# Moving attention steps later behind a head's results, and a fourth early pair with low parts on GpSimd

## The chip, the cores and the metric

The kernel runs on one core of a Trainium2 chip. The metric is the time of one execution on the device in microseconds (us). A core has TensorE (PE), which multiplies; VectorE (DVE) and ScalarE (ACT), which do elementwise work; GpSimd (POOL), which does elementwise work and issues some DMAs; and SyncE (SP), which issues most DMAs.

## The reference

Two layers over 768 tokens (a sequence of 512 and one of 256) of width 2048. The change lies at the end of layer 0 and in layer 1, whose core is this:

```python
h = x @ odd_w_in[i]
q, k, v, g = jnp.split(h, 4, axis=-1)
y = (_dilated_mixture(q, k, v, pos) * jax.nn.silu(g)) @ odd_w_out[i]
...
x = _layernorm(DN_ALPHA * x + y, ln_g[layer], ln_b[layer])
```

`_dilated_mixture` turns q and k of 16 heads by a rotary embedding on a quarter of each head's 128 dimensions, takes scaled scores inside three dilated windows, a softmax for each, and mixes the three results by their log sums. The kernel does the three windows as one softmax with an additive table.

## The kernel before

All products are made in three: an f32 matrix is split into a high part (a cast on ACT, L441) and a low part (a subtraction on DVE or POOL, L442), and high times high, high times low and low times high are summed in PSUM. The low parts of weights in the early products are made by the engine that `c.weng` names.

Layer 1's input projection runs in the class `Seven`: groups n = 0 to 63, each with seven products i = 0 to 6 of Strassen's kind, 448 in all. A product is 12 matmuls of 128 x 384 (L747). The operands of the tokens are sums and differences of quarters of the layer's input, made by `sums` in `turn0` (L1202 to L1217); those of the weights are made by `prep` (L722). A product's result is copied or added into the group's result tiles on ACT (L754, L756) and DVE (L752). Product (n, 6) completes a group, and stands behind the first product of group n + 1.

Groups below 32 leave half sums in DRAM; groups from 32 on add them and hand the results to attention. Two stretches matter:

- **The opening**, where layer 0's last block still ends. `n_first` groups have two of their products, (n, 0) and (n, 3), run "alone" ahead of the rest, since those need only quarters that are there early; their weights are split by `wtile`. Their results wait in `early` tiles. The other products follow in `seq`, with two more blocks of operands prepared in between.
- **The heads**, groups 32 to 63. A group of kind 0 or 2 holds q and k of one head, kind 1 holds v and kind 3 the gates of two heads. When (n, 6) of a kind 0 or 2 is done, `ready1` sends 32 rows to another tile by four DMAs (`rope_in`, L1396, POOL queue), turns them on DVE (`rope`, L1401 to L1405) and sends them back by four DMAs (L1407, POOL queue); then `parts` splits q and k into `qh`, `ql`, `kh`, `kl` (L441 on ACT, L442 on DVE), each of which has one buffer. Then come six attention steps (`Attn.step`): scores of one block of 128 queries (L838, three matmuls into `ps_sc`), the softmax, transposes of an earlier block (L870) and values of a pair of blocks (L883, `ps_o`). The last two blocks' transposes and values fall into the next head's first steps.

The order is written by hand through a queue: `later(c, i, f)` runs f at product i behind the one that completes a group, and `fill` takes what is due after each product. Two groups make a head's period, so 14 products lie between the results of one head and those of the next. The Tile framework's list scheduler then lays the instructions of each engine into one fixed order, in which each engine waits for whatever its next instruction needs.

After the last product, the output projection of layer 1 starts with its first block (`proj_t`, L578), inside which the last head's steps run.

Of the kernel before, what the change touches and what calls it, by code (L numbers as in the profile page):

```python
# [4 lines left out]
F32 = mybir.dt.float32  # L5
# [3 lines left out]
ALU = mybir.AluOpType  # L9
# [425 lines left out]
HALF = 384  # L435
# [43 lines left out]
def later(c, n, f):  # L479

    c.at.append((c.now + n, f))
    c.at.sort(key=lambda x: x[0])
# [196 lines left out]
class Seven:  # L679
# [31 lines left out]
    def split(self, n, i, raw):  # L711
        c = self.c
        hi, lo = (p.tile([128, 512], F32R, tag="w" + x, name="w" + x) for x, p in (("h", c.whi), ("l", c.wlo)))
        split_sb(c.nc, raw, hi, lo, c.nc.vector)
        self.hl[n, i] = tuple(a.rearrange("p (k f) -> p k f", k=4) for a in (hi, lo))
# [194 lines left out]
def hybrid_kernel(tc, x_p, x_s, w_in0, w_out0, a_re, a_im, log_dt, b_re, b_im, c_re, c_im, d_sk, glu_w, glu_b,  # L910
                  qn_g, kn_g, w_in1, w_out1, ln_g, ln_b, c_ident, c_eye, c_rope0, c_rope1, c_mix, out_p, out_s):
    from contextlib import ExitStack
    nc = tc.nc
    PS, DR = bass.MemoryType.PSUM, bass.MemoryType.DRAM
    with ExitStack() as es:
        pool = lambda n, b, **k: es.enter_context(tc.tile_pool(name=n, bufs=b, **k))
        rpool = lambda n: tc.tile_pool(name=n, bufs=1, side="right")
        c = Ctx()
# [56 lines left out]
        with rpool("lng") as lng:  # L975
# [10 lines left out]
            with rpool("tab") as tab:  # L986
# [5 lines left out]
                for b in range(8):  # L992
                    ps = start if b == 0 else proj_f(c, [(w0, 128 * b)], 16)
# [27 lines left out]
                    else:  # L1021
                        banks, _ = proj_t(c, w0, 3328, 256, range(16))
# [7 lines left out]
                        kbanks, _ = proj_t(c, w0, 3072, 256, range(16))  # L1030
# [136 lines left out]
        with rpool("po") as po:  # L1167
# [3 lines left out]
            def turn0(t):  # L1171
                mv = row_stats(c, po, stats, t)
                for x in (0, 1024):
                    b = slice(x, x + 1024)
                    nc.vector.tensor_scalar(out=z[:, t, b], in0=z[:, t, b], scalar1=mv[:, 0:1], scalar2=mv[:, 1:2],
                                            op0=ALU.subtract, op1=ALU.mult)
                    nc.gpsimd.dma_start(nd[:, t, b], z[:, t, b])
                tok = slice(128 * t, 128 * t + 128)

                def four(k0):  # L1180
                    ps = ps_tile(c, "ps_n")
                    for i in range(4):
                        nc.tensor.transpose(ps[:, 128 * i:128 * i + 128], z[:, t, 128 * (k0 + i):128 * (k0 + i) + 128], c.ident)
                    p = ps.rearrange("p (k n) -> p k n", k=4)
                    up = lambda a: a[:, k0:k0 + 4].unsqueeze(2).to_broadcast([128, 4, 128])
                    raw = z[:, t, 128 * k0:128 * k0 + 512].rearrange("p (k n) -> p k n", k=4)
                    parts = k0 == 4 or (k0 == 0 and t < 3)
                    for i in range(4):
                        k = k0 + i
                        nc.scalar.activation(out=c.xh[k][:, tok] if parts else raw[:, i], in_=p[:, i], func=AF.Identity,  # L1190
                                             scale=lgT[:, k:k + 1], bias=lbT[:, k:k + 1])
                    if not parts:
                        rest()
                        return
                    nc.vector.tensor_tensor(out=raw, in0=p, in1=up(lgT), op=ALU.mult)
                    nc.gpsimd.tensor_tensor(out=raw, in0=raw, in1=up(lbT), op=ALU.add)
                    rest(lambda: nc.vector.tensor_tensor(out=xl[:, k0:k0 + 4, tok], in0=raw,
                                                         in1=xh[:, k0:k0 + 4, tok].bitcast(F32), op=ALU.subtract))

                def sums():  # L1200

                    rest()  # L1202
                    u = t - 3
                    a11, a12, a21, a22 = (z[:, a, b:b + 512] for a in (u, t) for b in (0, 512))
                    tu = slice(128 * u, 128 * u + 128)
                    tt = lambda o, a, b, op: nc.vector.tensor_tensor(out=o, in0=a, in1=b, op=op)
                    tt(a22, a21, a22, ALU.add)
                    tt(a21, a11, a21, ALU.subtract)
                    tt(a11, a22, a11, ALU.subtract)
                    parts = [(raw.rearrange("p (k n) -> p k n", k=4), xh[:, k0:k0 + 4, s], xl[:, k0:k0 + 4, s])  # L1210
                             for raw, k0, s in ((a11, 0, tok), (a22, 8, tu), (a21, 8, tok), (a12, 12, tu))]
                    for raw, h, _ in parts[0:3]:
                        nc.scalar.copy(h, raw)
                    tt(a12, a12, a11, ALU.subtract)
                    nc.scalar.copy(parts[3][1], parts[3][0])
                    for raw, h, lo in parts:
                        tt(lo, raw, h.bitcast(F32), ALU.subtract)  # L1217

                ks = lambda x: [lambda k0=k0: four(k0) for k0 in x]
                if t < 3:  # L1220
                    c.q += ks((0, 4, 8, 12))
                else:
                    c.q += ks((4, 0)) + [sums]
                    late.extend(ks((8, 12)))

            left, late = [], []

            def rest(f=None):

# [27 lines left out]
            half = lambda k0, t0: tuple(lambda k, x=x: x[:, k0 + k, 128 * t0:128 * t0 + HALF] for x in (xh, xl))  # L1257
            ops = half(0, 0), half(0, 3), half(8, 0), half(4, 0), half(8, 3), half(12, 0)
            ops = [ops + (half(4, 3),), ops + (half(12, 3),)]
            n_first = 3  # L1260
            wes = es.enter_context(ExitStack())
            pw = wes.enter_context(tc.tile_pool(name="pw", bufs=1))
            free, whole = [z[:, t, 0:768] for t in range(6)], {}
# [2 lines left out]
            def outs(n):  # L1266
                two = lambda f: [f[:, 0:HALF], f[:, HALF:768]]
                if n >= 32:
                    return places[0](n)
                if n < n_first:  # L1270
                    return [early.tile([128, HALF], F32, tag="early", name="early", bufs=2 * n_first) for _ in range(2)]
                whole[n] = free.pop(0), free.pop(0)
                free.extend(whole[n])
                return two(whole[n][0]) + two(whole[n][1])
# [14 lines left out]
            products = sv.run(seq + sv.order(32, 64, 32), lambda: fill(c))  # L1289
            with rpool("early") as early:  # L1290
                c.q.append(rest)
                for n in range(n_first):
                    for i in (0, 3):
                        sv.alone(n, i, lambda: fill(c, 2))
                flush(c)
                for n in range(n_first):
                    f = free.pop(0)
                    free.append(f)
                    sv.res[n] += [f[:, 0:HALF], f[:, HALF:768]]
                c.q += late + [rest]  # L1300
                for m in range(seq.index((n_first - 1, 6)) + 1):
                    next(products)
                flush(c)
            with rpool("sx") as sx:
# [18 lines left out]
                for m in range(seq.index((n_first - 1, 6)) + 1, n_seq):  # L1323
                    n, i = next(products)
# [16 lines left out]
        with rpool("pc") as pc:  # L1341
# [13 lines left out]
            def ready1(n, r):  # L1355
                n -= 32
                t = heads1.pop(n + 32)
                flat = t.rearrange("p a n -> p (a n)")
                blocks = flat[:, 0:TOK], flat[:, TOK:2 * TOK]
                j, kind = n // 4, n % 4  # L1360
                two = hds[2 * j:2 * j + 2]
                if kind in (0, 2):
                    hd = two[kind // 2]
                    rt = rope_in(t)
                    nc.gpsimd.dma_start(flat[32:128], pd1[n, 32:128], accum_op=ALU.add)
                    later(c, 3, lambda: rope(t, rt, before.pop()))

                    def go():
                        hd.qq, hd.kk = parts(blocks[0], "q"), parts(blocks[1], "k")
                        att.add(hd)  # L1370

                    later(c, 6, go)
                    for i in (7, 8, 9, 10, 12, 13) if n < 30 else range(7, 16):
                        later(c, i, att.step)
                    if n < 30:
                        later(c, 6, lambda: before.append(rope_before(n + 2)))
                    return
                nc.gpsimd.dma_start(flat, pd1[n], accum_op=ALU.add)
                if kind == 1:
                    for i in range(2):  # L1380
                        later(c, 4 + i, lambda i=i: turn_v(blocks[i], two[i]))
                else:
                    for i in range(2):
                        later(c, 4 + i, lambda i=i: gate_sb(blocks[i], two[i], i))
# [29 lines left out]
            def turn_v(t, hd):  # L1414

                i = hd.h % 2
                assert hd.h < 2 or hds[hd.h - 2].ended
                vv = [a[:, 4 + 2 * i:6 + 2 * i, HALF:TOK].rearrange("p a (t f) -> p a t f", t=3) for a in (xh, xl)]
                hd.vv = vv
                for a in range(2):  # L1420
                    ps = ps_tile(c, "ps_v")[:, 0:HALF]
                    for b in range(3):
                        nc.tensor.transpose(ps[:, 128 * b:128 * b + 128], t[:, HALF * a + 128 * b:HALF * a + 128 * b + 128], c.ident)
                    split_ps(nc, ps.rearrange("p (t f) -> p t f", t=3), vv[0][:, a], vv[1][:, a])
# [172 lines left out]
```

## Time and profile before

| | us |
|---|---|
| median of 3 runs | 2727.89 (2725.62 to 2732.53) |
| the profiled execution | 2727.51 |
| its span, from first to last instruction | 2725.7 |
| PE busy | 2570.4 (94%) |
| DVE busy | 1822.6 (67%) |
| ACT busy | 1034.4 (38%) |
| POOL busy | 757.4 (28%) |

Times in the rows are microseconds from the span's start. The opening is at 1249 to 1293 us, groups 3 to 31 run until about 1740 us, the heads' attention fills 1762 to 2410 us, and the end of attention inside the output projection reaches 2461 us. In a row of the timeline stand the start, the length, engine, line, operation and tiles (out<-in); a bracket gives the idle time of the engine in front of the instruction and what ended it. Consecutive matmuls overlap, so the distance between starts, not the length shown, is what one costs.

### The profile page before, as it was taken

What the parts mean: (1) busy time and instruction counts of PE and PEld (TensorE: products, weight loads), DVE (VectorE), ACT (ScalarE), POOL (GpSimd) and SP (SyncE); (2) the same over time, 40 slices, a digit from 0 to 9 for tenths busy, and PEclk for the clock granted to TensorE, in tenths of its full rate; (3) what the DMA queues carried; (4) which work ended last, traced back from release to release, by engine and by line L of the source; (5) the groups of instructions that cost most, each with busy time, mean ns of one, the idle gap of its engine ahead of it and who ended that gap; (6) DMA issues with size and microseconds to landing.
All of it is one profiled execution on the core that took longest, in us unless ns stands there. A gap on an engine that the chain in (4) does not pass through costs nothing.

```text
span 2725.7 us, 42003 instructions
## 1 busy us (share of the span) xinstructions
PE 2570.4 (94%) x15632; PEld 2449.1 (90%) x15632; DVE 1822.6 (67%) x3588; ACT 1034.4 (38%) x2054; POOL 757.4 (28%) x649
## 2 busy tenths in 40 slices
PE   8899999998998999998999999999999999979997
PEld 7899999998997898887999999999999989978886
DVE  6578888858357742238766666877777777763437
ACT  4222222222335521127333333455555555551111
POOL 2645555536554430002000000011211111134404
PEclk9999999999999999998999999999999999989998
DMA  5333333332434362225334434444444444455222
GB/s 149 115 91 93 98 93 98 89 76 79 125 122 139 117 217 70 64 87 166 123 119 134 130 116 136 132 96 116 108 106 105 99 103 104 104 160 187 80 66 112
DMA packets 352107, 308.06 MB, mean 113 GB/s; under 512 B 60320, under 2 KB 303520, under 8 KB 351008
## 3 DMA queue, kind: packets, MB, share of 16 engines
q1 hardware_dynamic: 331856, 265.30, 32.1%
q0 software_dynamic: 10688, 36.71, 6.6%
q10 hardware_dynamic: 9360, 3.38, 0.8%
q8 instruction: 123, 2.02, 0.3%
q14 instruction: 80, 0.66, 0.1%
HBM read 231.58 MB, written 67.44 MB: 110 GB/s over the span
## 4 chain that ended last, share of the span: by engine, by line
PE 60%; DVE 19%; DMA 8%; issue 5%; ACT 3%; POOL 3%; SPq 2%; DVEq 0%; ACTq 0%; POOLq 0%
PE pt L578 22%; PE ps_y L747 11%; PE ps_z L747 6%; PE ps_x L747 6%; PE pa L534 4%; PE pb L534 3%; DMA b<-in_odd_w_in_dram 3%; PE ps_o L883 2%; PE ps_sc L838 2%; DVE wl L442 2%; DVE tmpv L227 1%; DVE res L752 1%; PE ps_pt L870 1%; DMA res<-rt 1%; POOL wl L442 1%
## 5 line engine op out<-in xcount | busy, mean ns | idle before, releaser
L441 ACT CAST wh<-wr 128x512 fp32r<-128x512 f32 x346 | 214.5, 624 | 663.9 <-PE pt L578 340.3
L578 PE MATMUL pt<-wh,xh 128*128 128x256 f32 (+1 forms) x1392 | 459.0, 330 | 6.4 <-ACT wh L441 6.4
L578 PE MATMUL pt<-wl,xh 128*128 128x256 f32 (+1 forms) x1392 | 457.3, 329 | 1.5 <-POOL wl L442 1.3
L578 PE MATMUL pt<-wh,xl 128*128 128x256 f32 (+1 forms) x1392 | 456.7, 328 | 0.0
L442 POOL TENSOR_TENSOR wl<-wr,wh 128x512 fp32r<-128x512 f32 x168 | 232.3, 1394 | 349.7 <-ACT wh L441 317.0
L442 DVE TENSOR_TENSOR wl<-wr,wh 128x512 fp32r<-128x512 f32 x178 | 148.5, 837 | 257.0 <-ACT wh L441 256.9
L578 PEld LDWEIGHTS pt<-wh,xh 128*128 128x128 f32 x1392 | 266.2, 192 | 30.2 <-ACT wh L441 7.2
L578 PEld LDWEIGHTS pt<-wl,xh 128*128 128x128 f32 x1392 | 266.7, 192 | 24.5 <-POOL wl L442 1.8
L578 PEld LDWEIGHTS pt<-wh,xl 128*128 128x128 f32 x1392 | 266.5, 191 | 22.7
L747 PE MATMUL ps_y<-xh,wh 128*128 128x384 f32 x768 | 262.7, 342 | 2.8 <-DVE res L752 1.7
L747 PE MATMUL ps_y<-xl,wh 128*128 128x384 f32 x768 | 258.4, 337 | 0.0
L747 PE MATMUL ps_y<-xh,wl 128*128 128x384 f32 x768 | 258.3, 336 | 0.0
L441 ACT CAST wh<-b 128x512 fp32r<-128x512 f32 x250 | 154.9, 620 | 216.4 <-PE ps_z L747 108.1
L442 DVE TENSOR_TENSOR wl<-b,wh 128x512 fp32r<-128x512 f32 x250 | 172.2, 689 | 44.0 <-ACT wh L441 43.8
L747 PE MATMUL ps_x<-xh,wl 128*128 128x384 f32 x512 | 172.9, 338 | 8.3 <-DVE wl L442 8.3
L534 PE MATMUL pa<-xh,wh 128*128 128x384 f32 x448 | 160.4, 359 | 20.0 <-ACT wh L441 16.7
L747 PE MATMUL ps_x<-xh,wh 128*128 128x384 f32 x512 | 175.8, 343 | 2.7 <-ACT early L754 1.6
L747 PE MATMUL ps_z<-xh,wh 128*128 128x384 f32 x512 | 174.1, 340 | 0.0
L747 PE MATMUL ps_x<-xl,wh 128*128 128x384 f32 x512 | 172.5, 337 | 0.0
L747 PE MATMUL ps_z<-xl,wh 128*128 128x384 f32 x512 | 171.3, 335 | 0.0
L747 PE MATMUL ps_z<-xh,wl 128*128 128x384 f32 x512 | 171.2, 334 | 0.0
L534 PE MATMUL pa<-xh,wl 128*128 128x384 f32 x448 | 154.2, 344 | 10.1 <-POOL wl L442 9.9
(359 smaller groups left out, 6401.6 us busy)
## 6 DMA issues: line engine op xcount, KB each, us to landing
b<-in_odd_w_in_dram SPq DMA_DIRECT2D x256, 256.0 KB, 2.9
wr<-in_even_w_in_dram SPq DMA_DIRECT2D x144, 256.0 KB, 3.3
pd<-z SPq DMA_DIRECT2D x58, 384.0 KB, 2.5
wr<-in_even_w_out_dram SPq DMA_DIRECT2D x64, 256.0 KB, 2.8
wr<-in_odd_w_out_dram SPq DMA_DIRECT2D x64, 256.0 KB, 3.2
res<-pd POOLq DMA_DIRECT2D x16, 768.0 KB, 6.9
res<-pd POOLq DMA_DIRECT2D x16, 576.0 KB, 6.5
nd<-z POOLq DMA_DIRECT2D x12, 512.0 KB, 4.5
```

The costliest lines, as they stand in the source:

```text
L227: e.tensor_tensor(out=tmp, in0=pt(9 + j), in1=xt(sx), op=ALU.mult)
L441: nc.scalar.copy(hi, src)
L442: (eng or nc.gpsimd).tensor_tensor(out=lo, in0=src, in1=hi.bitcast(F32), op=ALU.subtract)
L534: nc.tensor.matmul(out[n][s][:, 0:HALF], wt[:, j], xt[k][:, HALF * s:HALF * s + HALF], start=k == k0 and i == 0, stop=k == nk - 1 and i == 2)
L578: nc.tensor.matmul(view[t], xt[k][:, tok], wt[:, j], start=first and i == 0 and ti % per == 0, stop=last and i == 2 and ends)
L747: nc.tensor.matmul(ps, w[:, k], x(k), start=i < 3 and k == j == 0, stop=k == 3 and j == 2, skip_group_check=i >= 3)
L752: add = lambda o, b: nc.vector.tensor_tensor(out=r[o], in0=ps, in1=r[b], op=ALU.add)
L838: nc.tensor.matmul(s, a[:, qs], b[:, ks], start=j == 0, stop=j == 2)
L870: nc.tensor.transpose(ps[:, 128 * j:128 * j + 128], seq.ps[i][:, 128 * j:128 * j + 128], c.ident)
L883: nc.tensor.matmul(o, a, b[:, j], start=j == 0 and x == 0, stop=j == nt - 1 and x == 2)
```

## The change

Five things are altered.

1. `sums` splits its first two quarters first and puts the other sum and two splits into a list `second`, which is run behind the alone products.
2. `n_first` is 4 rather than 3: eight alone products stand ahead of the rest. Group 0 gets four early tiles.
3. During the alone products `c.weng` is GpSimd, so the low parts of their eight weights are made there.
4. A head's six steps stand at products 8, 10, 12, 15, 17 and 19 behind its results instead of 7, 8, 9, 10, 12 and 13. For the last head they stand at 8 to 16 instead of 7 to 15.
5. The transposes of v stand one product later (5 + i for 4 + i).

```diff
-                    for raw, h, _ in parts[0:3]:
-                        nc.scalar.copy(h, raw)
-                    tt(a12, a12, a11, ALU.subtract)
-                    nc.scalar.copy(parts[3][1], parts[3][0])
-                    for raw, h, lo in parts:
-                        tt(lo, raw, h.bitcast(F32), ALU.subtract)
+                    def split(ps):
+                        for raw, h, _ in ps:
+                            nc.scalar.copy(h, raw)
+                        for raw, h, lo in ps:
+                            tt(lo, raw, h.bitcast(F32), ALU.subtract)
+
+                    def more():
+                        tt(a12, a12, a11, ALU.subtract)
+                        split(parts[2:])
+
+                    split(parts[:2])
+                    second.append(more)
...
-            n_first = 3
+            n_first = 4
...
-                    return [early.tile([128, HALF], F32, tag="early", name="early", bufs=2 * n_first) for _ in range(2)]
+                    return [early.tile([128, HALF], F32, tag="early", name="early", bufs=2 * n_first + 2)
+                            for _ in range(4 if n == 0 else 2)]
...
                 c.q.append(rest)
+                c.weng = nc.gpsimd
                 for n in range(n_first):
                     for i in (0, 3):
                         sv.alone(n, i, lambda: fill(c, 2))
                 flush(c)
-                for n in range(n_first):
+                for n in range(1, n_first):
...
-                c.q += late + [rest]
+                c.weng = nc.vector
+                c.q += [lambda: [f() for f in second]] + late + [rest]
...
-                    for i in (7, 8, 9, 10, 12, 13) if n < 30 else range(7, 16):
+                    for i in (8, 10, 12, 15, 17, 19) if n < 30 else range(8, 17):
                         later(c, i, att.step)
...
-                        later(c, 4 + i, lambda i=i: turn_v(blocks[i], two[i]))
+                        later(c, 5 + i, lambda i=i: turn_v(blocks[i], two[i]))
```

On PE, at the first score of the second head, the instructions before the change stood like this (the first row is the last matmul of a product; `ps_o` are values of the head before, `ps_y` the next product):

```order
L747 MATMUL ps_x<-xh,wl 128x384
L838 MATMUL ps_sc<-kh,qh 128x512
L883 MATMUL ps_o<-pth,xh 128x256
L883 MATMUL ps_o<-ptl,xh 128x256
L883 MATMUL ps_o<-pth,xl 128x256
...
L838 MATMUL ps_sc<-kl,qh 128x512
L838 MATMUL ps_sc<-kh,ql 128x512
...
L870 MATMUL ps_pt<-ident,pp 128x128 x2
L747 MATMUL ps_y<-xh,wh 128x384
```

In the changed kernel, from the head before's last step, three products ahead of that score:

```order
L838 MATMUL ps_sc<-kh,ql 128x256
L870 MATMUL ps_pt<-ident,pp 128x128 x4
L747 MATMUL ps_z<-xh,wh 128x384
...
L747 MATMUL ps_y<-xh,wl 128x384
L838 MATMUL ps_sc<-kh,qh 128x512
L838 MATMUL ps_sc<-kl,qh 128x512
L838 MATMUL ps_sc<-kh,ql 128x512
L883 MATMUL ps_o<-pth,xh 128x256
...
L870 MATMUL ps_pt<-ident,pp 128x128 x2
L747 MATMUL ps_y<-xh,wh 128x384
```

The score stands one product later, and three steps of the head before (at its products 15, 17 and 19) now lie between that head's successor's results and this score, where before there were products alone; the three score matmuls are together, with the values behind all of them.

On POOL, at the opening, `wl` are low parts of weights, `nd<-z` are stores, and the other two lines belong to the end of layer 0. Before:

```order
L906 TENSOR_TENSOR mv<-mv,mhalf 128x1
L1196 TENSOR_TENSOR z<-z,lbT 128x512
L1177 DMA nd<-z 128x1024 x2
L1196 TENSOR_TENSOR z<-z,lbT 128x512
L1338 DMA lrow<-in_ln_g_dram 128x256
```

In the changed kernel:

```order
L906 TENSOR_TENSOR mv<-mv,mhalf 128x1
L442 TENSOR_TENSOR wl<-wr,wh 128x512
L1196 TENSOR_TENSOR z<-z,lbT 128x512
L1177 DMA nd<-z 128x1024 x2
L442 TENSOR_TENSOR wl<-wr,wh 128x512 x2
L1196 TENSOR_TENSOR z<-z,lbT 128x512
L442 TENSOR_TENSOR wl<-wr,wh 128x512
L1347 DMA lrow<-in_ln_g_dram 128x256
```

The last four of the eight low parts stand here among the other work; the first four stand further up, ahead of POOL's first `mv`. On DVE they are gone.

## Rows read from the trace of the kernel before

**Rows 1.** Waits of PE, 1722 to 2411 us: total us, times, longest.

```profile
PE ps_sc L838 <- ACT kh L441: 25.0, 14, 3.0
PE ps_o L883 <- ACT xh L446: 2.5, 4, 1.4
PE ps_sc L838 <- issue: 2.2, 1, 2.2
```

**Rows 2.** Windows: from:to, us, busy of PE, PEld, DVE, ACT, POOL, granted clock, DMA.

```profile
1265.60:1282.70 17.10, 11.24 (x34) 10.03 (x35) 16.38 (x27) 8.23 (x16) 0.00 (x0) 0.50 0.25 71
1310.00:1740.00 430.00, 430.00 (x2482) 429.86 (x2481) 296.19 (x486) 159.62 (x277) 0.00 (x0) 1.00 0.40 125
1762.80:2408.70 645.90, 610.96 (x3636) 589.53 (x3635) 487.50 (x1004) 365.14 (x751) 115.27 (x166) 0.98 0.43 105
1770.80:1774.20 3.40, 3.40 (x12) 3.21 (x11) 2.88 (x6) 0.39 (x2) 0.00 (x0) 0.50 0.41 116
2327.00:2330.50 3.50, 3.50 (x15) 3.40 (x14) 2.01 (x6) 1.63 (x5) 0.00 (x0) 0.52 0.49 146
```

**Rows 3.** Timeline of the second head, results to first score (columns as described above).

```profile
1797.02 0.56 DVE L752 TENSOR_TENSOR res<-ps_y,res 128x384 f32<-128x384 f32 x1 [0.91 <-PE ps_y L747]
...
1803.26 0.55 DVE L1405 TENSOR_TENSOR rt<-rt,sh 128x384 f32<-128x384 f32 x1
...
1804.10 2.00 POOL L1407 DMA_DIRECT2D res<-rt  x4 [4.87 <-DVE rt L1405]
...
1809.60 0.83 ACT L441 CAST qh<-res 128x768 fp32r<-128x768 f32 x1 [3.82 <-DMA res<-rt]
...
1810.86 0.83 ACT L441 CAST kh<-res 128x768 fp32r<-128x768 f32 x1
...
1811.74 0.79 PE L838 MATMUL ps_sc<-kh,qh 128*128 128x512 f32 x1 [2.28 <-ACT kh L441]
...
1811.94 0.95 DVE L442 TENSOR_TENSOR kl<-res,kh 128x768 fp32r<-128x768 f32 x1
```

**Rows 4.** Timeline of PE: the first head's fifth and sixth step.

```profile
1786.90 0.28 PE L838 MATMUL ps_sc<-kh,qh 128*128 128x256 f32 x1
...
1789.12 0.82 PE L1423 MATMUL ps_v<-ident,res 128*128 128x128 f32 x6
...
1791.86 0.28 PE L838 MATMUL ps_sc<-kh,qh 128*128 128x256 f32 x1
...
1792.57 0.42 PE L747 MATMUL ps_x<-xh,wh 128*128 128x384 f32 x1
```

**Rows 5.** Timeline of PE at the opening.

```profile
1260.87 0.42 PE L747 MATMUL ps_x<-xh,wh 128*128 128x384 f32 x1
...
1269.81 0.69 PE L747 MATMUL ps_x<-xh,wl 128*128 128x384 f32 x1 [8.34 <-DVE wl L442]
...
1279.23 0.69 PE L747 MATMUL ps_y<-xh,wh 128*128 128x384 f32 x1 [1.08 <-ACT wh L441]
```

**Rows 6.** Timeline of DVE and POOL at the opening.

```profile
1221.99 1.44 POOL L906 TENSOR_TENSOR mv<-mv,mhalf 128x1 f32<-128x1 f32 x2 [231.89 <-DVE mv L905]
...
1262.98 1.41 POOL L1196 TENSOR_TENSOR z<-z,lbT 128x512 f32<-128x512 f32 x1 [5.26 <-DVE z L1195]
...
1263.80 1.14 DVE L1206 TENSOR_TENSOR xl<-z,xh 128x512 fp32r<-128x512 f32 x1 [0.31 <-ACT xh L1213]
...
1269.07 0.68 DVE L442 TENSOR_TENSOR wl<-wr,wh 128x512 fp32r<-128x512 f32 x1
```

**Rows 7.** Groups of the page: busy us, mean ns of one, idle before.

```profile
L442 POOL TENSOR_TENSOR wl<-wr,wh 128x512 fp32r<-128x512 f32 x168 | 232.3, 1394 | 349.7 <-ACT wh L441 317.0
```

**Rows 8.** Timeline of the last head, POOL, DVE and PE.

```profile
2410.71 3.44 POOL L1339 TENSOR_TENSOR res<-res,lrow 128x1536 f32<-128x1536 f32 x1
2411.07 5.60 DVE L442 TENSOR_TENSOR xl<-res,xh 128x768 fp32r<-128x768 f32 x1 [2.53 <-ACT xh L441]
...
2423.97 0.79 PE L838 MATMUL ps_sc<-kl,qh 128*128 128x512 f32 x1 [7.05 <-DVE kl L442]
```

More of the change, by code (lines that the diff above doesn't have):

```diff
@@ L1224, in turn0 @@
                     late.extend(ks((8, 12)))
-            left, late = [], []
+            left, late, second = [], [], []
             def rest(f=None):
```

## The prediction

> **What bounds the kernel now.** I read the page's busy shares first: PE is busy for nearly the whole span, so time can only be had where PE waits, or where it runs at the lower clock. I then asked for the waits of PE stage by stage, and for the clock by windows. Between the opening and the heads PE has no idle time at all: 2482 matmuls in 430 us, 0.173 us each, so a product of 12 costs 2.08 us [rows 2]. Nothing in the change can gain there. Two stretches are left in which PE waits and which the change touches.
>
> In the heads, PE waits 25.0 us in 14 waits for the cast `kh` in front of a head's first score, and once 2.2 us more at the same place with no releaser shown [rows 1]; that is 15 of 16 heads, one wait each, and the sixteenth is at the end. It waits another 2.5 us for v's high part. The granted clock of the stretch of 1762.8 to 2408.7 us is 0.98 [rows 2]: after seven of these waits the clock stood at half for about 3.4 us, of which the first and the last are shown at 0.50 and 0.52. Half of 3.4 us is lost in each, 1.7 us, in all 12 us, which agrees with 2% of 645.9 us (12.9 us).
>
> At the opening PE stands still for 8.34 us within one alone product, for a weight's low part that DVE makes at 1269.07, after a long run of sums (L1206) in program order [rows 5, 6]. DVE does not idle there, 16.38 of 17.10 us, and the clock is at 0.50 through the whole of 1265.6 to 1282.7 [rows 2].
>
> **The heads: the chain and its cover.** The second head shows the chain [rows 3]. The last sum of its results starts at 1797.02, just as its product ends. The rotary work on DVE ends with the operation at 1803.26, the four DMAs back are issued from 1804.10 to 1806.1, the high part of q starts at 1809.60 when they have landed, that of k at 1810.86, and the score at 1811.74. From 1797.0 to the end of `kh` at 1811.7 are 14.7 us, to the end of `kl` at 1812.9 (0.95 from 1811.94) 15.9. PE reached the score 2.28 us early, at 1809.46: its cover is 12.5 us, six products. The order of before explains it: nothing but products stands there.
>
> In the changed order a seventh product stands in front, 2.08 us, and three steps of the head before. From the trace, the fifth step takes 1786.90 to 1789.12, 2.2 us, and the sixth 1791.86 to 1792.57, 0.7 us [rows 4]; the fourth, three scores of 512 columns and four transposes, I estimate from these at 1.0 us. So the cover grows by 2.08 + 3.9 = 6.0 us, to 18.5. Before, the values of the last head could also go between the first score's matmuls; now all three are together, so it is `kl` that must be there: 15.9 us here, and for the longest wait (3.0 us) 12.5 + 3.0 + 1.2 = 16.7 us. That leaves 1.8 to 2.6 us to spare. Into this go new hindrances: three steps' DVE and ACT work now lies in the same 18.5 us. A step brings DVE a masked score, a low part of a transpose and a reciprocal, by the 0.68 us that an operation on 512 columns takes [rows 6] about 1.6 us, so up to 4.8 us, of which only what stands in front of the five rotary operations or of the splits delays the chain. I take it that half of the heads wait about 1 us, 8 us in all.
>
> Removable are 25.0 + 2.2 + 2.5 us of waits and 12 us of clock, 41.7 us. The transposes of v move back by one product, but the first values move back by five, so that wait goes. Of the clock I keep 1 us, since the half clock came behind waits of about 2 us and more. The net is 41.7 - 8 - 1 = **about 33 us**. The bounds: 8 us if the steps' work fills the spare time and most waits come back, 42 us if none does.
>
> The gate product on POOL (o times g) now stands between the second and third of the four DMAs that start the rotary work. It lies ahead of the last result in time, and the fourth DMA waits for that result anyway, so I cost it at nothing; if the cover fails, it adds its own length, under 2 us, to each head's chain, and that is inside the spare time.
>
> **The opening.** The 8.34 us wait goes, as the low part no longer queues on DVE. POOL is free for it: it idles 231.89 us up to 1221.99, where the first four low parts now stand, and 5.26 us ahead of 1262.98 [rows 6]; one costs it 1.39 us [rows 7]. From 1260.87 four alone products, 8.3 us, can run back to back in the new order, plus about 1.6 us of waits for ACT's copies (an estimate from the 1.08 us in front of 1279.23), so that the rest starts at about 1270.9 rather than 1279.23 [rows 5]: 8.3 us. Two more products are then done, another 2 x 2.08 = 4.2 us. Against this stand about 1.5 us for the parts of a21, which are now made later than before (two operations of 0.68 us on DVE). So far 11.0 us. The clock should not fall, which would save about 1.7 us of the remaining 3.5 us at half clock after 1279.23; I set against it 1.8 us for DVE work slowed by POOL, worked out below. The term is **about 11 us**, with bounds of 5 (a wait of half the old length returns further on) and 15 us (no new waits).
>
> The deduction for POOL has a row: the low part on DVE at 1263.80 took 1.14 us under a POOL operation at 1262.98, where its like takes 0.68 [rows 6], and in the tail one of 128 x 768 took 5.60 us under L1339 [rows 8], against 0.95 in [rows 3]. The Trainium skill (GPSIMD Engine Reference, Key points) says that GpSimd shares its interfaces to SBUF with VectorE, and that DVE instructions with two SBUF inputs contend there. All subtractions of the opening are of that kind, so the rule speaks against this part of the change, and the trace agrees with it. By the milder row the four low parts in the busy stretch cost 4 x 0.46 = 1.8 us, by the worse one 4 x 4.65 = 18.6 us, 16.8 us more, and the opening would lose 6 us rather than gain 11. I take the milder one, since it is from this place and this shape.
>
> **The tail.** The last head waits 7.05 us for `kl`, which stands on DVE behind the 5.60 us operation [rows 8]. Its steps move by one product and in the new order its rotary DMAs no longer stand behind a low part on POOL, but GpSimd's residual work stays. I take 3 us of gain, between -4 (the wait moves, and a longer row of steps is left behind the last product) and 10 (it goes).
>
> **Sum.** 33 + 11 + 3 = 47 us. The profiled execution took 2727.51, 1.8 us over its span and 0.4 below the median of 2727.89, so the two need no correction: about **2681 us**.
>
> **Rivals.**
>
> *Steps crowd the rotary chain.* DVE is busy for 487.5 of 645.9 us in the heads [rows 2], and a head of 43.06 us (645.9 / 15) would shrink to 41; the share rises from 75 to 80%. If the three steps delay each chain by 3 to 4 us, half of the waits and of the clock's 12 us remain: gain 15 in place of 33, in all 28, 2700 us. For it: the chain has five DVE operations in a queue that also waits for PE's scores. Against it: its own waits are on DMA landings, with 3.5 us from the last issue to `qh`, which no engine's queue can lengthen.
>
> *GpSimd takes from DVE what it gives to PE.* The opening's term becomes -6 as worked out above, the rest stands: 33 + 3 - 6 = 30, 2698 us. For it the 5.60 us row, against it the 1.14 us one.
>
> *The heads give nothing.* The waits turn up at other instructions, such as low parts of weights behind the steps' DVE work: only the opening and the tail are left, about 11 us, 2716 us, and a little less gain would be no change that can be told.
>
> *Slower: q and k have one buffer each.* The last score of a head now stands four products behind the next head's results, at 4 x 2.08 + 2.2 + 1.0 + 0.4 = about 12 us, and the casts of that head's q and k, at 12.6 us (1809.60 - 1797.0), must wait for it. If the score comes later than its place, `qh` waits in ACT's queue with the next weights' high parts behind it, PE waits for these, and the score comes later still. It decides from a delay of about 0.6 us on; to cost more than all the gains it has to take 47 / 15 = 3.1 us from each head, and with 4 us each the time is 2728 - 47 + 60 = 2741 us. For it: the slack is small. Against it: PE, on which it depends, would be the engine that waits for nothing there, and a late cast still has the rest of 18.5 us.
>
> **How the numbers follow.** The forecast has 0.62, the crowded chain 0.16, GpSimd's contention 0.06, nothing from the heads 0.10, slower 0.06. The forecast's own range is 2664 to 2697, from 64 us (15 + 42 + 7) to 30 us of gain. Taking in the first two rivals and most of the third gives 2664 to 2714. A measurement of this kernel can tell about 0.3%, 8 us, from no change. The first three cases are faster by more, and 0.06 of the fourth: 0.90. The other 0.04 of it and 0.01 of the last are the same: 0.05. Slower is 0.05.
>
> **What would show it.** The opening: no wait above 2 us in the alone products, the first `ps_y` product near 1271 us, and the clock at 1.00 before 1283. The heads: waits for `kh` and `kl` below 10 us in all, a head period of about 41 us, and the clock at 0.99 or more in that stretch. The chain itself should still take about 15 to 17 us; if it takes over 18.5 the crowding rival holds. `qh` should start on a DMA's landing, not on a score: if on a score, the one buffer decides. If DVE's low parts of 128 x 512 take over 2 us at the opening, GpSimd's contention was mis-sized. The forecast is wrong if the heads' period is still 43 us.

## The result and the profile after

The changed kernel takes 2679.61 us (median of 4 runs, 2678.12 to 2683.31), the kernel before beside it 2726.94 (4 runs). The ratio is 0.9825, 95% interval [0.9807, 0.9842]: 47 us faster, against 47 forecast (2681). The sum is right, but not all of its terms are, and the profiles show why.

The profiled execution took 2678.12 us, its span 2676.3. PE's waits in the heads' stretch are now these (us in total, times, longest), which answer [rows 1]:

```profile
PE ps_o L883 <- DVE ptl L447: 3.1, 4, 1.2
PE ps_sc L838 <- DVE kl L442: 2.9, 4, 1.1
PE ps_x L747 <- DVE sst L845: 0.5, 1, 0.5
```

No wait for `kh` is left, and `kl` has taken its place at four heads, for 2.9 us against 27.2. Of the other waits, the one for v's high part is gone, and one for `ptl` has grown from 0.8 to 3.1 us. To compare stretches whose work is the same I cut both traces at products: the 1st product's first matmul, the 41st's, the 232nd's and the last one's. The windows of the heads' stretch (232nd to last) are, before and after (columns as in [rows 2]):

```profile
1753.42:2408.21 654.79, 619.86 (x3687) 598.42 (x3687) 494.02 (x1017) 369.01 (x758) 116.21 (x167) 0.98 0.44 105
```

```profile
1756.43:2363.41 606.98, 600.41 (x3687) 587.52 (x3687) 496.75 (x1014) 356.65 (x755) 119.26 (x172) 1.00 0.47 114
```

The same 3687 matmuls take 47.8 us less. PE's idle time fell from 34.9 to 6.6 us (28.4), and its busy time by 19.4, of which 11.9 is the seven half-clock stretches: the clock is 1.00 now. The other 7.5 us of busy time lie around the scores. Outside the half-clock stretches, with listed waits taken off, the mean distance between starts within the products is 0.177 us in both traces. From a product to a score it is 0.174 us instead of 0.202 (90 times), from a score to values 0.193 instead of 0.261 (52 times before), and among values 0.122 instead of 0.134 (341 times before). That is 10 us together, a little of which other places take back; why values are spaced wider beside a wait stays open.

The second head again, as in [rows 3]:

```profile
1794.01 0.56 DVE L752 TENSOR_TENSOR res<-ps_y,res 128x384 f32<-128x384 f32 x1
...
1802.69 1.02 POOL L1416 DMA_DIRECT2D res<-rt  x2 [6.47 <-DVE rt L1414]
...
1806.26 0.84 ACT L441 CAST qh<-res 128x768 fp32r<-128x768 f32 x1 [0.27 <-DMA res<-rt]
...
1807.96 0.84 ACT L441 CAST kh<-res 128x768 fp32r<-128x768 f32 x1
...
1809.17 0.95 DVE L442 TENSOR_TENSOR kl<-res,kh 128x768 fp32r<-128x768 f32 x1
...
1812.40 0.39 PE L838 MATMUL ps_sc<-kh,qh 128*128 128x512 f32 x1
```

From the results to the end of `kl` are 16.1 us (15.9 before), and PE comes after 18.4 (12.5 before), with nothing in brackets, which means no idle time. So the chain did not get faster; PE only comes to it later, with work of the head before in between.

At the opening the waits are shorter, 6.6 us in all against 11.0, but not gone. Of PE (its start, length, and in brackets what it waited for):

```profile
1269.24 0.45 PE L747 MATMUL ps_x<-xh,wh 128*128 128x384 f32 x1 [1.40 <-ACT early L754]
...
1282.43 0.69 PE L747 MATMUL ps_x<-xh,wh 128*128 128x384 f32 x1 [3.54 <-ACT early L754]
```

and of ACT, POOL and DVE ahead of the second one:

```profile
1277.91 1.63 POOL L442 TENSOR_TENSOR wl<-wr,wh 128x512 fp32r<-128x512 f32 x1 [2.46 <-issue]
```

```profile
1278.33 1.76 DVE L1206 TENSOR_TENSOR z<-z 128x512 f32<-128x512 f32 x1
```

```profile
1280.18 0.62 ACT L1214 CAST xh<-z 128x512 fp32r<-128x512 f32 x1 [1.35 <-DVE z L1206]
1280.71 0.47 ACT L756 COPY early<-ps_x 128x384 f32<-128x384 f32 x1
1281.38 0.62 ACT L1214 CAST xh<-z 128x512 fp32r<-128x512 f32 x1 [0.21 <-DVE z L1206]
1281.91 0.47 ACT L754 COPY early<-ps_x 128x384 f32<-128x384 f32 x1
```

The copy that PE waits for needs nothing but PE's own result, yet in ACT's order it stands behind a cast that waits for a sum on DVE, and that sum is slowed by the low part on POOL (1.76 us instead of 0.68). The wait of [rows 5] for `wl` has become a wait for ACT, passed on from DVE.

Stretch by stretch, in us; the last two rows are means over profiles of the experiments below, so that single executions count for less:

| | start to 1st product | 1st to 41st | 41st to 232nd | 232nd to last | last product to end |
|---|---|---|---|---|---|
| before | 1249.6 | 104.9 | 399.0 | 654.8 | 317.5 |
| after | 1259.6 | 98.1 | 398.8 | 607.0 | 312.9 |
| attention as before (3 profiles) | | | | 655.7 | 317.3 |
| opening as before (6), as after with either engine (6) | 1254.5, 1257.6 | 103.7, 96.8 | | | |

The first column is not the change's: up to there all kernels have the same instructions in the same order on every engine but for a few low parts and one weight's load at its very end, and still the first product begins anywhere from 1249.6 to 1262.0 us in the fourteen profiles. The changed kernel's profile had lost its 10.0 us already at the matmul that stands nine tenths of the way (1125.0 against 1115.0 us), ahead of every instruction that differs. This hid part of its gain in that execution.

### The profile page after: what moved, and what is told of

It reads as the page before. It is cut to its first block, busy times and chain, and to the rows that moved or that the text cites. A ratio compares the mean times of both kernels' runs of the same rounds, so it can differ in the third digit from the quotient of the medians.

```text
span 2676.3 us, 42003 instructions
## 1 busy us (share of the span) xinstructions
PE 2550.7 (95%) x15632; PEld 2437.6 (91%) x15632; DVE 1823.4 (68%) x3580; ACT 1021.4 (38%) x2054; POOL 767.5 (29%) x657
## 4 chain that ended last, share of the span: by engine, by line
PE 61%; DVE 20%; DMA 7%; issue 4%; POOL 3%; ACT 2%; SPq 2%; DVEq 0%; ACTq 0%; POOLq 0%
PE pt L578 21%; PE ps_y L747 12%; PE ps_z L747 7%; PE ps_x L747 7%; PE pa L534 3%; PE pb L534 3%; PE ps_o L883 2%; PE ps_sc L838 2%; DMA res<-pd 2%; DVE wl L442 2%; DVE tmpv L227 1%; PE ps_pt L870 1%; DMA wr<-in_even_w_in_dram 1%; POOL wl L442 1%; DVE res L752 1%
## 5 line engine op out<-in xcount | busy, mean ns | idle before, releaser
L442 POOL TENSOR_TENSOR wl<-wr,wh 128x512 fp32r<-128x512 f32 x176 | 242.6, 1388 | 581.0 <-ACT wh L441 538.2
```

Source lines behind the costliest of these rows:

```text
L442: (eng or nc.gpsimd).tensor_tensor(out=lo, in0=src, in1=hi.bitcast(F32), op=ALU.subtract)
```

## The experiments

All ratios are to runs of the kernel before, made beside each run on the same chip. The last three columns are stretches of one profile each, in us.

| run | ratio, 95% interval | 1st to 41st | 232nd to last | last to end |
|---|---|---|---|---|
| 1 attention edits alone | 0.9847 [0.9830, 0.9864] | 103.2 | 613.3 | 314.2 |
| 2 opening edits alone | 0.9992 [0.9978, 1.0006] | 96.8 | 658.2 | 316.2 |
| 3 after, low parts on DVE | 0.9813 [0.9798, 0.9828] | 96.1 | 609.2 | 313.7 |
| 4 after, steps later but not spread | 0.9931 [0.9916, 0.9946] | 97.1 | 636.7 | 317.9 |
| 5 run 1, steps spread but not later | 0.9926 [0.9904, 0.9949] | 103.3 | 638.0 | 312.3 |
| 6 run 1, steps one product later still | 0.9880 [0.9854, 0.9906] | 103.2 | 624.4 | 320.8 |
| 7 run 1, v's transposes back | 0.9847 [0.9825, 0.9870] | 103.3 | 613.6 | 317.0 |
| 8 before, ten early tiles | 0.9991 [0.9979, 1.0003] | 104.0 | 654.1 | 318.2 |
| 9 after, sums' order alone of the opening | 0.9837 [0.9819, 0.9854] | 100.3 | 610.2 | 318.1 |
| 10 after, fourth pair alone of the opening | 0.9852 [0.9836, 0.9867] | 102.5 | 609.2 | 317.2 |
| 11 after, residual operations later | 0.9819 [0.9804, 0.9833] | 95.7 | 611.9 | 317.5 |
| 12 after, last gates later | 0.9823 [0.9797, 0.9848] | 97.1 | 610.7 | 316.0 |

### Which part gives the time: runs 1 and 2

Run 1 has the two attention lines of the diff in the kernel before; run 2 has the changed kernel with these two taken back.

> The kernel before with only the attention steps and the transposes of v moved. Theory A, from the two traces (the heads gave 48 us and the tail 5, the opening 7, and 10 us were lost ahead of the opening by chance): 2675 us, 2672 to 2680, with under 8 us of waits in the heads and no half clock there. Theory B, the prediction's sizes (33 in the heads, 3 in the tail): 2691 us. Theory C, the 10 us lost ahead of the opening come with this part: 2685 us.

> The changed kernel with the attention steps and the transposes of v as before, so only the opening's three edits. Theory A (opening gains about 7 us, upstream loss by chance): 2720 us, 2717 to 2723. Theory B (the prediction's 11): 2716 us. Theory C (the opening's edits bring the 10 us lost ahead of it, for instance by another layout of SBUF): 2728 to 2731 us, and the first alone product begins near 1259 us instead of 1249.6.

Run 1 is 42 us faster than before (0.0153 of 2731), run 2 at most 6 us, its interval holds no change at all. So nearly all of the gain is the attention steps'. Run 1's time, 2686 us, is theory C's, but not for its reason: the first product began at 1252.3 us, so the 10 us were not lost there. (The kernel before took 2731 us beside it, 4 us more than the theories reckoned with, and theory A's 48 us of the heads came out lower.) Its stretches show where the gain lies: 41.5 us in the heads with 10.5 us of idle time and no half clock, 3.3 in the tail. Run 2's opening is 8.0 us shorter than the before's, but its time of 2729 us and its first product at 1261.6 us looked like theory C.

The opening's 7 us are seen in the totals only on top of the new steps: the kernels with the new steps have 0.9847 twice with the opening of before (runs 1 and 7) and 0.9813 to 0.9825 with that of after (after, runs 3, 11 and 12). That run 2 shows none of them stays open; in its one profile the heads took 658.2 us, 3.4 more than before.

### Is the loss ahead of the opening the opening's? Run 8, and run 7 by chance

The code is shown from the middle of its line.

```diff
-bufs=2 * n_first) for _ in range(2)]
+bufs=2 * n_first + 4) for _ in range(2)]
```

> The kernel before with ten early tiles in place of six, of which the last four are not used: the same instructions, another size of one pool. Theory A (the 7 to 12 us that all four kernels with the opening's edits lose ahead of the opening come from where tiles lie): the first alone product begins at 1256 to 1261 us and the time is 6 us or more over that of before. Theory B (they come with the edited instructions or by chance): it begins at 1249 to 1253 us, and the time is that of before within 4 us.

The first product began at 1252.9 us and the time was that of before, theory B. Then run 7, which has the opening of before, began at 1262.0. So a late start needs none of the opening's edits: executions differ by some 12 us in this stretch with nothing changed. In run 7 PE's busy time up to the first product was 5.7 us longer than in the before's profile (1179.6 against 1173.9), its idle time 6.7 us longer, and the clock stood at half for 71.7 us rather than 58.0; what sets this off stays open. The means of the two openings, 1254.5 and 1257.6, lie closer than the single profiles, and these runs do not tell whether 3 us of it come with the edits.

### One product later, or spread? Runs 4, 5 and 6

Each run alters the one tuple of the steps (shown cut, with the run's number added behind #).

```diff
-(8, 10, 12, 15, 17, 19) if n < 30
+(8, 9, 10, 11, 13, 14) if n < 30      # run 4
+(7, 9, 11, 14, 16, 18) if n < 30      # run 5
+(9, 11, 13, 16, 18, 20) if n < 30     # run 6
```

> The changed kernel with the steps at 8, 9, 10, 11, 13, 14: one product later than before, but together. Theory A (three steps of the head before are 3.9 of the 6.0 us of new cover, and kl needs 15.9 to 16.7 us against a cover of 14.6): waits of 1.3 to 2.1 us at nearly every head, 20 to 30 us in all, some half clock, 2700 to 2712 us. Theory B (the one product is enough, and the spread only thins DVE's work): waits under 8 us in all, 2678 to 2684 us.

> The first experiment (attention edits alone) with the steps at 7, 9, 11, 14, 16 and 18: spread, but not later. Theory A (cover is what counts: 12.5 + 3.9 = 16.4 us against a chain of 15.9 to 16.7 to kl): waits for kh and kl of 0 to 1.5 us a head, 5 to 15 us in all, no wait for pth, 2690 to 2700 us. Theory B (the one product later is needed and the spread only keeps other waits away): waits for kh and kl over 20 us in all, 2705 us or more.

> The first experiment with the steps at 9, 11, 13, 16, 18 and 20, one more product later, so that the last score of a head stands five products (10.4 us) and two steps behind the next head's results, about 14 us, while its q lands after 12.6. Theory A: qh waits for that score, 1 to 2 us a head, but kl is still there before a cover of 20.6 us: waits for kl under 2 us in all, 2680 to 2687 us. Theory B (the prediction's slower rival: the wait of qh blocks ACT's queue and with it the weights): waits of 1 us or more a head at products (L747) or scores, 2700 us or more.

I worked out for each trace, as means over 15 heads, when `kl` is done and when PE would come to the first score. The first two rows count from the start of the last sum of a head's results on DVE, the next two from the end on PE of the product that completes these results (its last matmul's start and 0.17 us).

| us | before | run 4, later | run 5, spread | after, both | run 6 |
|---|---|---|---|---|---|
| `kl` done | 14.9 | 15.1 | 15.5 | 16.8 | 17.5 |
| PE comes | 11.8 | 14.3 | 13.3 | 17.0 | 18.7 |
| `kl` done, from the product | 15.7 | 15.5 | 17.6 | 18.3 | 19.4 |
| PE comes, from the product | 12.6 | 14.7 | 15.4 | 18.5 | 20.6 |
| ratio | 1 | 0.9931 | 0.9926 | 0.9825 | 0.9880 |

Either half alone gives less than half of the gain, and each leaves PE ahead of `kl`. Run 5 has theory B's time and waits. My 16.4 us of cover were wrong: a step at product 14 stands ahead of the product that completes the next head's results, so it is no cover for them, and 15.4 is what was left. The last sum, moreover, stands on DVE behind that step's softmax and starts 2.1 us behind its product (0.8 before, 1.5 after), which delays the chain, so 13.3 are left from the sum. Its waits in the heads:

```profile
PE ps_sc L838 <- DVE kl L442: 18.7, 15, 1.6
PE ps_sc L838 <- ACT kh L441: 5.5, 5, 2.0
PE ps_sc L838 <- issue: 1.2, 1, 1.2
```

Run 4 came out at theory A's time, but for another reason than the one given: the waits for `kl` are 6.6 us only, and 14.0 us are seven new ones, at every second head, for the high part of a transpose:

```profile
PE ps_o L883 <- ACT pth L446: 14.0, 7, 2.3
PE ps_sc L838 <- DVE kl L442: 6.6, 9, 1.4
```

The first of them shows where it comes from; the other six stand alike. ACT's rows:

```profile
1820.62 0.84 ACT L1437 ACTIVATE g<-res 128x768 f32<-128x768 f32 x1 [3.71 <-DMA res<-pd]
1821.37 0.35 ACT L446 CAST pth<-ps_pt 128x256 fp32r<-128x256 f32 x1
```

and PE's:

```profile
1821.78 0.38 PE L883 MATMUL ps_o<-pth,xh 128*128 128x256 f32 x1 [2.01 <-ACT pth L446]
```

The transpose on PE was done, but its cast stands in ACT's order behind the gate's Tanh, which waits 3.71 us for a DMA (3.59 to 3.95 us at the other six). PE pays for a DMA that it does not use. With the steps spread, in the changed kernel, no wait of PE for `pth` is left in the heads.

Run 6 has cover in plenty and is slower than run 1 by 9 us by the ratios (0.0033); in the two profiles it is 11 us in the heads and 7 in the tail. At six of the 16 heads `qh` starts 2.1 to 2.6 us later than its data, here 2.4 us behind the landing of the second of the four DMAs back, the last that q needs, at 1889.4. The head before's last score reads the `qh` that is overwritten with its first two matmuls, which start on PE at 1891.29 and 1891.41; but `qh` also stands behind a weight's cast that waits for PE, so these rows do not tell the one buffer, my slower rival, from the order:

```profile
1891.31 0.62 ACT L441 CAST wh<-b 128x512 fp32r<-128x512 f32 x1 [1.46 <-PE ps_z L747]
1891.84 0.83 ACT L441 CAST qh<-res 128x768 fp32r<-128x768 f32 x1
```

But that is not what PE waits for at the scores: waits for `kl` are 1.1 us. The new waits are v's transposes for DVE and for a DMA (5.8 and 2.8 us) and products for results' sums on DVE (4.1 and 1.7), that is, other work of the same queues pushed together, plus 6.2 us for `kh` at the last head. The time is in theory B's range, but the waits are not those that it names, so neither theory held.

### v's transposes: run 7

```diff
-                        later(c, 5 + i, lambda i=i: turn_v(blocks[i], two[i]))
+                        later(c, 4 + i, lambda i=i: turn_v(blocks[i], two[i]))
```

> The first experiment with the transposes of v at 4 + i again. Theory A: the first values stand five products later than v, so one product there is worth nothing: 2683 to 2690 us, like the first experiment. Theory B (v's work on DVE and ACT collides with a step's when it stands one product earlier): waits for ptl or pth grow by over 5 us, 2692 us or more.

The ratio is run 1's, 0.9847, and the heads' stretch 613.6 against 613.3: that edit is worth nothing. (Its absolute time of 2694 us is theory B's, but the kernel before took 2733 beside it, and the waits that theory B names did not grow.) There are 5.4 us of waits of v's transposes for the DMA that brings v, and 3.7 us less of waits for `ptl` than in run 1.

### The opening's three edits: runs 3, 9 and 10

Run 3 leaves out `c.weng = nc.gpsimd`; runs 9 and 10 do so too, and have `n_first = 3`, and `more()` called at once, respectively.

> The changed kernel with the eight low parts of the alone products on DVE again. Theory A (GpSimd's operations stretch DVE's by about 4 us in all in the opening, which is as much as the 8 low parts cost on DVE): 2678 to 2682 us, and DVE's operations of 512 columns all near 0.68 us. Theory B (without GpSimd a low part queues behind the sums again): 2685 to 2690 us, with a wait of PE for DVE wl of 4 us or more among the alone products.

> The changed kernel with three pairs ahead (n_first 3) and the low parts on DVE, so of the opening's edits only the sums put first are left. The stretch from the first alone product to the 41st product takes 103.6 us with the old opening and 97.0 with the new (means of six and four profiles). Theory A (what the low part of the fifth weight waited for on DVE was the long row of sums, so putting two of them first gives the gain): 97 to 99.5 us in that stretch and no wait over 3 us for wl. Theory B (the fourth pair covers the sums' time): 101 us or more. The whole time follows it by no more than 3 us: 2678 to 2686.

> The changed kernel with four pairs ahead, the low parts on DVE and the sums whole again. Theory A (the sums' order gives the gain): the stretch takes 101 us or more, with a wait for wl of 5 us or more. Theory B (the fourth pair gives it): 96 to 99 us, since two more products of 2.1 us stand where PE waited.

GpSimd's part is worth nothing, and run 3's time is theory A's: 96.1 us with all low parts on DVE, 95.7 to 98.1 with them on GpSimd. Run 9's gain of 3.3 us and run 10's of 1.2 us (against 103.7) do not add up to the 6.8 us of both. Each edit alone leaves its own wait, run 9's behind the last alone product, where the rest's first weights are not ready, run 10's at the low part again:

```profile
1278.01 0.69 PE L747 MATMUL ps_y<-xh,wh 128*128 128x384 f32 x1 [5.26 <-ACT wh L441]
```

```profile
1274.93 0.69 PE L747 MATMUL ps_x<-xh,wl 128*128 128x384 f32 x1 [4.24 <-DVE wl L442]
```

As I read these waits, the shorter sums let the low parts come early, and the fourth pair then fills the time that the deferred sums need. Run 9's 100.3 us lie between its two theories, 0.8 and 0.7 us off; run 10's 102.5 us are theory A's, with a wait for `wl` of 4.24 us where I expected 5 or more. I had taken it that one of the two would be the cause.

### The tail: runs 11 and 12

In the changed kernel the tail's longest wait has the same cause as run 4's, here of ACT and then of PE:

```profile
2383.53 0.84 ACT L1437 ACTIVATE g<-res 128x768 f32<-128x768 f32 x1 [3.62 <-DMA res<-pd]
2384.30 0.83 ACT L441 CAST xh<-res 128x768 fp32r<-128x768 f32 x1
2385.04 0.37 ACT L446 CAST pth<-ps_pt 128x256 fp32r<-128x256 f32 x1
```

```profile
2385.46 0.58 PE L883 MATMUL ps_o<-pth,xh 128*128 128x256 f32 x1 [5.59 <-ACT pth L446]
```

Run 11 loads the two rows of the residual operations into one tile of the kind that head 14's output leaves, so that POOL does them behind the gates' DMA:

```diff
-            residual1(pc, res0, 0)
...
+            row = pc.tile([128, TOK], F32, tag="o1", name="o1", bufs=2)
+            for i, (src, op) in enumerate(((ln_g, ALU.mult), (ln_b, ALU.add))):
...
```

> The changed kernel with GpSimd's two residual operations on res0 (3.5 us each) moved behind the DMA that brings the last group's gates. Theory A (in the tail PE's 5.6 us wait for pth comes from ACT's queue, where the gate's Tanh waits for a DMA that POOL issues behind these two, and ql on DVE takes 5.07 us beside the first of them): the gates land about 7 us earlier, ql takes under 2.5 us, the tail from the last product to the end is 6 to 12 us shorter than 312.9, and the time 2668 to 2674. Theory B (something else in the tail holds PE, such as the md loads): under 3 us.

`ql` fell from 5.07 to 2.15 us and the wait for `kl` went, but of the gates, counted from the last product's start, the DMA is issued 8.3 us on rather than 12.6 and the Tanh starts 18.3 us on rather than 20.1. PE waits 7.22 us for `pth` at the same place and 4.19 at another, and the tail is no shorter (317.5), as theory B has it. Run 12 takes the Tanh itself out of the way:

```diff
+                elif n == 31:
+                    two[1].gates = lambda z: [gate_sb(blocks[i], two[i], i, z) for i in range(2)]
...
-                nc.scalar.activation(out=g, in_=t, func=AF.Tanh, scale=0.5)
+                nc.scalar.activation(out=g, in_=t, func=AF.Tanh, bias=z, scale=0.5)
...
+                    if self.h == 15 and t0 == 0:
+                        z = pc.tile([128, 1], F32, tag="zb", name="zb", bufs=1)
+                        nc.vector.tensor_scalar(out=z, in0=self.o[:, 0:1], scalar1=0.0, scalar2=None, op0=ALU.mult)
+                        self.gates(z)
```

> The changed kernel with the Tanh of the last group's gates (ACT) put behind the last head's first values, by a bias of zero that is made from them, so that in ACT's queue it no longer stands ahead of that head's pth. Theory A (in the tail PE's 5.6 us wait for pth is the wait of this Tanh for its DMA, passed on by ACT's order): the wait for pth falls under 2 us at that place, the tail from the last product to the end is 4 to 9 us shorter than 312.9, and the time 2671 to 2677 us. Theory B (the md loads or the transposes hold that place anyway, or the gates' result tile, held longer, delays the md loads): the tail changes by under 3 us or grows, 2677 us or more.

Theory B holds: the next DMA in ACT's order, for the output projection's operands, takes the place, and PE waits 6.08 us where it waited 5.59:

```profile
2384.31 0.83 ACT L441 CAST xh<-res 128x768 fp32r<-128x768 f32 x1 [4.54 <-DMA res<-md]
2385.05 0.61 ACT L441 CAST wh<-wr 128x512 fp32r<-128x512 f32 x1
2385.57 0.36 ACT L446 CAST pth<-ps_pt 128x256 fp32r<-128x256 f32 x1
```

None of the twelve is shown to beat the changed kernel; runs 3, 11 and 12 are its equals.

## Why the prediction was right, and where its terms were off

**The heads, 33 forecast, 46 to 48 measured** (47.8 in the two profiles, 46 in the mean of the five profiles named below; the eight with the new steps singly 42 to 49). The mechanism held in each step: the wait was for the rotary chain, PE's cover grew, `kl` became the one that binds, `qh` starts on a landing (0.10 to 0.15 us behind that of q's second DMA at all 16 heads, so the one buffer of the slower rival did not bind), and the half clock went with the waits. Counted from the product on PE, the cover is 18.5 us, as forecast, 5.8 more than before where I had 6.0. From there the steps' DVE and ACT work lengthened the chain by 2.6 us (15.7 to 18.3), as "new hindrances" said; 0.7 of this lie ahead of the last sum, which the forecast took to start with its product's end. The term that was mis-sized is the 8 us that half of the heads were to lose of it: `kl` costs 2.9 us. In the mean only 0.2 us are to spare, so the crowded-chain rival was near. Runs 4 and 5, with 0.8 and 2.2 us too little, lose 30 us in the heads against the changed kernel and 25 against run 1, though in run 4 14.0 us of that are the waits for `pth`. Beside the 5 us at `kl` the difference of 15 us between 47.8 and 33 is made of the 1 us of clock that I kept, of small waits (5.2 us that I left out, of which 3.7 are there again), and of the 7.5 us of busy time above. The seven half-clock stretches of before follow waits of 1.66 to 3.03 us, and a wait of 2.55 us has none behind it, so my "about 2 us and more" was no dividing line.

**The opening, 11 forecast, 6.8 measured.** The step that failed is that the low part's queue was all that held PE: four products were to run back to back with 1.6 us of waits. ACT's order held them for 1.40 and 3.54 us, behind casts that wait for DVE's sums, and for 0.46 behind layer 0's activations, and the clock fell to half for 6.8 us from 1280.9, which I had said it would not. The deduction for contention was too small: five DVE operations of 512 columns took 1.27 to 1.76 us beside POOL's. Four of them lie beside low parts, 3.4 us over their 0.68, where I had 1.8 by [rows 6]; the fifth lies beside an operation of layer 0's, of the kind that [rows 6] has in the kernel before. That is far from the 18.6 of [rows 8]. The row of [rows 6] was no price of a whole low part: POOL's operation had only 0.59 us left when DVE's began. The rows show that such a DVE operation is held until POOL's has ended:

```profile
1268.43 1.38 POOL L442 TENSOR_TENSOR wl<-wr,wh 128x512 fp32r<-128x512 f32 x1
```

```profile
1268.59 1.76 DVE L1206 TENSOR_TENSOR z<-z 128x512 f32<-128x512 f32 x1
```

It ends 0.54 us after POOL's; the others, the one of [rows 6] and the one at 1278.33 among them, end 0.53 to 0.55 us after. The Trainium skill's rule (GPSIMD Engine Reference, Key points), that GpSimd shares its interfaces to SBUF with VectorE, agrees with these rows. Run 3 shows what it comes to here: moving the low parts away from DVE gives nothing. There the four low parts in the busy stretch cost DVE 4 x 0.60 = 2.4 us from start to start, less than the 3.4 us that they cost it from the other engine, and the other four stand where DVE has time.

**The tail, 3 forecast, about 2 measured** (317.3 to a mean of 315.2 over five profiles with the new steps, runs 1, 3, 9, 10 and after). The 7.05 us wait of [rows 8] shrank to 2.1 us, and the waits for `pth` grew from 1.9 to 7.0.

**The sum.** That it came out to 1.4 us is luck: errors of 13 to 15 us in the heads and -4 and -1 in the others met an execution-to-execution spread as large as themselves. By stretches the gain is 46 + 7 + 2 = 55 us, or 52 with the later mean start of the first column, by timed medians 47. The range has a flaw of its own: the terms' bounds add up to gains of 9 and 67 us, not to the 30 and 64 that it goes by.

## What to carry to other kernels

When one engine waits at a fixed place for a chain that cannot be shortened, put other work of that engine between the chain's start and the place, and count as cover only what stands behind the start: a step on the boundary counts for nothing. Ask of every in-order engine what stands ahead of the instruction that is waited for; in the opening, in run 4 and in the tail, PE waited for a copy or a cast that had its data and stood behind one that did not. Compare kernels by stretches cut at the same instruction before believing a term of some us in the total.

## What was not expected of the hardware

A stretch of 1250 us with the same instructions in the same order took between 1249.6 and 1262.0 us in fourteen profiles, and the kernel before between 2723.8 and 2744.9 us in 13 runs on one chip. A change of 2 us cannot be seen in such totals, but in stretches it can: the 191 products from the 41st to the 232nd took 398.7 to 399.0 us in every profile.

A DVE subtraction or sum beside a GpSimd operation is not slowed evenly; it waits the other out. In the profile of the changed kernel 35 subtractions and sums of 128x512 on DVE took over 0.9 us (0.92 to 3.90, where 0.68 is usual), and every one ended 0.53 to 0.57 us after a GpSimd operation beside which it ran. What such an overlap costs is therefore the rest of GpSimd's operation, not a fixed surcharge.
